# Branches of a hybrid decoder step in another order, and later use of what comes last at its seams

## The chip, the cores and the metric

The kernel runs on one core of a Trainium2 chip, as one launch. The metric is the device time in microseconds (us). Three runs of the kernel before gave 1140.0 (median), 1137.69 and 1142.15. The core has a tensor engine (PE; its weight loads are listed apart as PEld), a vector engine (DVE), a scalar engine (ACT), GpSimd (POOL) and SyncE (SP), which issues most loads. Each works through its own queue in order; the tensor engine's results go to PSUM, which DVE and ACT read.

## The reference

Two layers of a decoder trunk are run for a prompt of 256 tokens and for 8 samples of 4 tokens, 288 columns in all, with 1024 rows of model width. Cut to what matters here:

```
h  = rms(x)
q,k,v, x_b,y_b, q_c,k_c,v_c,r_c, a_c, g_a,g_b,g_c = split(h @ w_in)
o_a = window attention with sinks(q, k, v)                # branch a
o_b = gelu(y_b) * rg_lru(conv4(x_b))                      # branch b: a recurrence
o_c = rms(gla(q_c, k_c, v_c, a_c)) * silu(r_c)            # branch c: linear attention
x += (sig(g_a)*(o_a@Wa) + sig(g_b)*(o_b@Wb) + sig(g_c)*(o_c@Wc)) @ w_out
x += softmax(rms(x_q) rms(mem_k)) mem_v @ Wo              # 4 heads, 256 memory tokens
x += (silu(g) * val) @ w_down,  g,val = conv3(rms(x) @ w_up)
```

The three products with Wa, Wb, Wc are added up, and a sum has no order that the result depends on beyond rounding.

## The kernel before

Activations lie with the model dimension on partitions: X and its two halves xh and xl are eight blocks (k = 0 to 7) of 128 x 288. Each large product is made from three matmuls in fp32r (`mm3`, L213 to L215): xh by the weight's high half, xl by its high half, xh by its low half. A weight tile of 128 x 1024 is loaded by SP into `wst`, ACT writes its high half `whi` (L142) and DVE its low half `wlo` (L143). There are four `wst` and three each of `whi` and `wlo`. A tile of w_in feeds eight blocks k, so 24 matmuls; two tiles fill one two-bank PSUM buffer (`mm`, two of them). Four single banks (`sm`) serve everything small.

**What sets the order.** The queue of PE is the order in which the program is written. The chains of the three branches (`swa`, `gla`, `lru`), the norms and the memory's rms are generators: each `yield` hands back to the projections, and `tick` (L179) lets a chain take its next step when a running estimate of PE's time, `est["pe"]`, has passed the chain's `ready`. `account` adds to that estimate for each instruction: n/2400 us and 0.012 for an fp32r matmul, n/600 for one in fp32. A step becomes ready 0.3 us, plus what its yield gives, after the estimated end of the last. On DVE, ACT, POOL and SP a scheduler sets the order from priorities (`high_priority`) and its own estimates.

**A layer.** `mixers` makes the projections with the three chains interleaved; the recurrence's chain starts when linear attention's is past its states, and holds its exponentials (L744) until `swa` is done. Then come the gates (`gate(x)`, 4 x 2 tiles, x = 0 window attention, 1 recurrence, 2 linear attention) and the branch products (`branch(x)`, four pairs m = 0, 2, 4, 6, of 24 matmuls each). `branch` first calls `finish` on its chain. DVE multiplies the gate by the product out of PSUM (L1461); the sum `acc` is added on POOL for x = 1 and for the first two pairs of x = 2, on DVE for the last two (L1463); after x = 2 each pair is split into the halves `bh`, `bl` (L227 on ACT, L228 on DVE). `residual` multiplies them by w_out; its first pair of outputs takes k = 0 to 5 of both outputs first, then 6 and 7. `cross` is the cross-attention; it ends with the transposes of the probabilities (L1220), the samples' 64 small products (L1262), their transpose (L1268), the prompt's values (L1274) and the products with Wo. `ffn` is unchanged but for its first pair of products.

The wait for the window attention in the recurrence and the branches' order before:

```
        while not active["swa"].done:
            yield
...
        gate(0)
        gate(1)
        branch(0)
        gate(2, (0, 2, 4))
        branch(1, (0, 2))
```

Of the kernel before, what the change touches and what calls it, by code (L numbers as in the profile page):

```python
# [16 lines left out]
P = 128  # L17
# [49 lines left out]
def trunk(ctx: ExitStack, tc: tile.TileContext, a: dict):  # L67
# [82 lines left out]
    def account(i):  # L150

        if not hasattr(i, "engine") or not i.outs or i.opcode == "DMACopy":
            return
        e, n = str(i.engine), 1
        for _, c in i.outs[0].ap[1:]:
            n *= c
        if i.opcode == "Matmult":
            rows, cols = i.ins[0].ap[0][1], 1
            for _, c in i.ins[1].ap[1:]:
                cols *= c  # L160
            if i.ins[0].dtype == F32R:
                c = n / 2400 + 0.012
            elif getattr(i, "is_transpose", False):
                c = 0.109
            else:
                c = n / 600 * min(1.0, -(-rows // 32) / 4) * min(1.0, -(-cols // 32) / 4)
            est["pe"] += c
            if est["cur"] is not None:
                est["cur"] = max(est["cur"], est["pe"])
            return  # L170
        c = {"EngineType.DVE": 0.09 + n / 970, "EngineType.Activation": 0.12 + n / 1200}.get(e, 0.15 + n / 600)
        f = str(getattr(i, "func", "")).split(".")[-1]
        if i.opcode == "Activation" and f in TABLES and est["table"] not in TABLES[f]:
            est["table"] = TABLES[f][0]
            c += 1.28
        cur = est["cur"] if est["cur"] is not None and est["serial"] else est["pe"]
        t = est["busy"][e] = max(est["busy"].get(e, 0.0), cur) + c
        if est["cur"] is not None and not (est["serial"] and e == "EngineType.Pool"):
            est["cur"] = max(est["cur"], t + 0.1)  # L179
# [37 lines left out]
    def proj(out, src, nk, bh, bl):  # L217

        hi, lo = weights(src)
        for k in range(nk):  # L220
            w = slice(k * P, (k + 1) * P)
            mm3(out, hi[:, w], lo[:, w], bh(k), bl(k), k == 0, k == nk - 1)
            if k % 2:
                tick()

    def split(hi, lo, src):
        A.copy(hi, src)  # L227
# [72 lines left out]
    def head_norm(src, n, scale, nt=T, bw=TB):  # L300

        sq = s5()[:, : n * nt].rearrange("p (j t) -> p j t", t=nt)
        A.activation(sq, src, AF.Square)
        yield
        pss = psm()
        for j in range(n):
            PE.matmul(pss[32 * j : 32 * j + 32, :nt], cc("one32"), sq[:, j], start=True, stop=True, skip_group_check=True)
        yield
        ss = m1(nt)
        A.copy(ss[: 32 * n], pss[: 32 * n, :nt])  # L310
        yield
        nb = nt // bw
        pt = psm()
        for b in range(nb):
            PE.transpose(pt[:bw, b * P : b * P + 32 * n], ss[: 32 * n, b * bw : (b + 1) * bw], ident[: 32 * n, : 32 * n])
        yield
        cols = pt[:bw, : nb * P].rearrange("p (b j g) -> p b j g", j=4, g=32)[:, :, :n, 0]
        v = sm([P, 32], "rc")[:bw, : nb * n]
        V.tensor_copy(v.rearrange("p (b j) -> p b j", j=n), cols)
        r = rsqrt(v, [bw, nb * n], scale)  # L320
        yield
        return r
# [157 lines left out]
    def swa(l, got, Q, KV):  # L480
# [37 lines left out]

            V.scalar_tensor_tensor(x, x, prm[:, l, g : g + 1], bc(cc(c), n), ALU.mult, ALU.mult)

        yield
        pq, pg = flip(ss, 2, P), psm()
        for b in range(3):
            PE.transpose(pg[:TB, b * 32 : b * 32 + 32], sk[:, b * TB : (b + 1) * TB], ident[:32, :32])
# [110 lines left out]
        for kv in range(2):  # L635
            rows = slice(kv * 64, kv * 64 + 64)
            G.tensor_copy(qblk[rows, :, kv, :, :], Q[rows, :, NP_:T].rearrange("p j (b s) -> p b j s", s=NS))
        yield
        pscore = psm()
        for b in range(NB):  # L640
            r = 32 * (b % 4)
# [7 lines left out]
        for g in range(2):  # L649
            V.tensor_tensor_reduce(out=pt[:, g, :], in0=pscore[:, g * 132 : g * 132 + 132], in1=cc("ms"),  # L650
                                   scale=rqs[:, g : g + 1], scalar=-3e38, op0=ALU.add, op1=ALU.max, accum_out=mx[:, g : g + 1])
        yield
        sink = prm[:, l, C_SKS : C_SKS + 1]
        V.tensor_scalar(mx, mx, sink, -1.0, ALU.max, ALU.mult)
        A.activation(es, mx, AF.Exp, bias=sink)
        for g in range(2):
            A.activation(pt[:, g, :], pt[:, g, :], AF.Exp, bias=mx[:, g : g + 1], accum_out=den[:, g : g + 1])
        yield
        V.tensor_add(den, den, es)
        V.reciprocal(den, den)  # L660
        for g in range(2):
# [3 lines left out]
        for g in range(2):  # L665
            V.tensor_mul(pn[:, g], pt[:, g, P : P + NS].unsqueeze(1).to_broadcast([P, NB, NS]),
                         mb[:, g].unsqueeze(2).to_broadcast([P, NB, NS]))
        yield
        ptr = psm()
        for g in range(2):  # L670
            PE.transpose(ptr[:, g * P : (g + 1) * P], pt[:, g, :P], ident)
            PE.transpose(ptr[:32, (2 + g) * P : (3 + g) * P], pn[:, g].rearrange("p b s -> p (b s)"), ident)
        yield
        ptt = m1(2 * P)
        ptn = m1(2 * P)[:32]
        A.copy(ptt, ptr[:, : 2 * P])
        V.tensor_copy(ptn, ptr[:32, 2 * P : 4 * P])
        yield
        po = psm()
        for g in range(2):  # L680
            PE.matmul(po[:, g * P : (g + 1) * P], ptn[:, g * P : (g + 1) * P], vs, start=(g == 0), stop=False,
# [1 line left out]
        for b in range(NB):  # L683
            r, g = 32 * (b % 4), b // 4
            PE.matmul(po[r : r + 32, g * P : (g + 1) * P], ptt[:, b * 32 : b * 32 + 32], vc[:, b, :], start=False, stop=True,
                      skip_group_check=True)
        yield
        ot = m1(2 * P)
        A.copy(ot, po[:, : 2 * P])
        yield  # L690
        po = psm()
        for g in range(2):
            PE.transpose(po[:, g * P : (g + 1) * P], ot[:, g * P : (g + 1) * P], ident)
        yield
        os = m1(P).rearrange("p (j t) -> p j t", j=4)
        pov = po[:, : 2 * P].rearrange("p (b v j s) -> p v j b s", v=2, j=4, s=NS)
        for kv in range(2):
# [11 lines left out]
    def lru(l, got, xb, gy):  # L709
# [23 lines left out]
        for t in range(4):  # L733
            for g, (dst, c) in enumerate(((r, C_LBA), (ig, C_LBX))):
                pg = psm()
                PE.matmul(pg[:, :WO], wax[:, g * 4 + t, :], xc[:, t], start=True, stop=True)
                A.activation(dst[:, t], pg[:, :WO], AF.Sigmoid, bias=prm[:, l, c + t : c + t + 1])
            yield
        while not active["swa"].done:
            yield  # L740
        av, u = s5w(), s5w()
        for t in range(4):
# [282 lines left out]
    def mem_rms(sqs):  # L1025

        if sqs:
            pss = psm()
            for k, sq in enumerate(sqs):
                PE.matmul(pss[32 * k : 32 * k + 32, :NP_], cc("one32"), sq, start=True, stop=True, skip_group_check=True)  # L1030
            ss = m1(NP_)
            A.copy(ss, pss[:, :NP_])
            yield
            pt = flip(ss, 2, P)
            sr = sm([P, 3], "sr")[:, :2]
            V.tensor_reduce(sr, pt[:, :, :, 0], AX.X, ALU.add)
            V.tensor_copy(rm, rsqrt(sr, [P, 2], 1.0 / D))
            yield
            pb = psm()
            for b in range(2):  # L1040
                PE.transpose(pb[:, b * P : (b + 1) * P], rm[:, b : b + 1].to_broadcast([P, P]), ident)
            A.copy(rmb, pb[:, :NP_])
# [42 lines left out]
    def residual(srcs, nks, bh, bl, out=None):  # L1085

        for m in range(0, KD, 2):
# [8 lines left out]
                for k in range(nks[c]):  # L1096
                    todo.append((i, offs[c] + k, hi[:, k * P : (k + 1) * P], lo[:, k * P : (k + 1) * P]))
            if m == 0 and nk_all == KD:
                todo.sort(key=lambda t: t[1] >= 6)

            split_ = out is not None and m == KD - 2
            po = [psm(), psm()] if split_ else [pm[:, 0], pm[:, 1]]
# [33 lines left out]
    def cross(l, mem, mh, ml, kcs, vcs):  # L1136
# [74 lines left out]
        def flips(b):  # L1211
# [2 lines left out]
            V.reciprocal(dn, dn)  # L1214
            for h in range(4):
                V.tensor_scalar(pt[:, h], pt[:, h], dn[:, h : h + 1], None, ALU.mult)
            for m in range(2):
                ptr = psm()
                for h in range(4):
                    PE.transpose(ptr[:, h * P : (h + 1) * P], pt[:, h, m * P : (m + 1) * P], ident)  # L1220
                dst = ptt[m][:, :, ts]
# [42 lines left out]
                              skip_group_check=True)  # L1264
        os = m1(P)
        A.copy(os, po[:, :P])
        ptr = psm()
        PE.transpose(ptr[:, :P], os, ident)  # L1268
        split(oh[:, :, NP_:T], ol[:, :, NP_:T], ptr[:, :P].rearrange("p (h t) -> p h t", t=32))
        for h in (0, 2):  # L1270
            po = psm()
            for i in range(2):
                for m in range(2):
# [2 lines left out]
            po3 = po.rearrange("p (h t) -> p h t", t=NP_)  # L1276
            split(oh[:, h : h + 2, :NP_], ol[:, h : h + 2, :NP_], po3)

        for m in range(0, KD, 2):
            hi, lo = weights(a["wo"][l, m // 2], 0 if m == 2 else AHEAD)  # L1280
            pm = pmm()
            for i in range(2):
                for k in range(4):
                    w = slice(k * 256 + i * P, k * 256 + (i + 1) * P)
                    mm3(pm[:, i, :T], hi[:, w], lo[:, w], oh[:, k], ol[:, k], k == 0, k == 3)
            with tc.high_priority(AHEAD):
                V.tensor_add(X[:, m : m + 2], X[:, m : m + 2], pm[:, :, :T])


    def ffn(l):  # L1290
# [7 lines left out]
        def up(c, pm=None):  # L1298
            if pm is None:
                pm = pmm()  # L1300
                pm = (pm, pm[:, 0], pm[:, 1])
            for i in range(2):
                proj(pm[1 + i][:, :T], a["up"][l, 2 * c + i], KD, lambda k: xh[:, k, :], lambda k: xl[:, k, :])
            return pm
# [45 lines left out]
    def mixers(l):  # L1350
        chains, got = active, {}

        def win(i, n):
            pm = pmm()
            for j in range(n):
                proj(pm[:, j, :T], a["win"][l, i + j], KD, lambda k: xh[:, k, :], lambda k: xl[:, k, :])
            return pm
# [91 lines left out]
        def branch(x, ms=range(0, KD, 2)):  # L1449
            oh, ol = chains[("swa", "lru", "gla")[x]].finish()  # L1450
            for m in ms:
# [7 lines left out]
                g = gates[x, m]  # L1459
                with tc.high_priority(AHEAD):  # L1460
                    V.tensor_mul(g, g, pm[:, :, :T])  # L1461
                if x:
                    (G if x == 1 or m < KD - 4 else V).tensor_add(acc[m], acc[m], g)  # L1463
                else:
                    acc[m] = g
                if x == 2:
                    w = slice(m % 4, m % 4 + 2)
                    split(bh[m // 4][:, w], bl[m // 4][:, w], acc[m])

        gate(0)  # L1470
        gate(1)
        branch(0)
        gate(2, (0, 2, 4))
        branch(1, (0, 2))
        mh = [s5v(4, NP_, F32R), s5v(4, NP_, F32R)]
        ml = [s5v(4, NP_, F32R), s5v(4, NP_, F32R)]
        mem = active["mem"] = Chain(mem_load(l, mh, ml))
        gate(2, (6,))
        branch(1, (4, 6))
        branch(2)  # L1480
        kcs = [load_kc(l, b) for b in range(NB)]
        vcs = [load_vc(l, b, g2) for b in range(4)]
        residual(lambda m: [a["wout"][l, m]], (KD,), lambda k: bh[k // 4][:, k % 4], lambda k: bl[k // 4][:, k % 4])
# [194 lines left out]
```

## Time and profile before

| | |
|---|---|
| three runs | 1140.0 us (1137.69 to 1142.15) |
| the profiled execution | 1141.05 us, its span 1139.1 us |
| PE busy, PEld busy | 1107.9 us (97%), 1061.3 us (93%) |
| DVE, ACT, POOL busy | 794.3 us (70%), 629.8 us (55%), 252.4 us (22%) |
| mean granted clock of PE | 0.989 |
| HBM | 172 GB/s over the span |

The span runs from the first instruction to the last; 1.95 us of the profiled execution lie around it. Busy is the union of an engine's instructions. Matmuls overlap and their ends are modelled, so the pace is read from starts or from counts in a stretch. In the rows, `<-` in a wait names what ended it.

### The profile page before, as it was taken

How to read it: one execution, taken by the hardware profiler on the slowest of the kernel's cores; microseconds unless marked ns; L12 is line 12 of the kernel's file. 1: busy time of each engine (PE TensorE's matmuls, PEld its weight loads, DVE VectorE, ACT ScalarE, POOL GpSimd, SP SyncE). 2: the span in 40 equal slices, each digit the busy share in tenths (PEclk: the TensorE clock that was granted, in tenths of full speed). 3: DMA queues.
4: the chain of work that ended last, by engine and by line, in shares of the span. 5: the costliest groups of instructions: out<-in, count | busy, mean ns of one | idle time of the engine just before them, and what ended most of it. 6: DMA issues, size and time to landing. Idle time of an engine off the chain costs nothing. (4 is left out here: it accounts for less than half of the span.)

```text
span 1139.1 us, 22360 instructions
## 1 busy us (share of the span) xinstructions
PE 1107.9 (97%) x8846; PEld 1061.3 (93%) x8846; DVE 794.3 (70%) x1454; ACT 629.8 (55%) x971; POOL 252.4 (22%) x426
## 2 busy tenths in 40 slices
PE   9999997999999999999999999979999999999998
PEld 8898986999988999999999989869999899999998
DVE  6876866777765887885458769566776668878743
ACT  6545777535455656654346476864354456566532
POOL 1220101031111455550022100010311014555400
PEclk9999998999999999999999999989999999999999
DMA  8753453567466555556555435445675544455662
GB/s 279 266 181 115 152 179 116 187 201 242 150 221 234 148 167 161 155 162 197 172 170 180 138 103 178 160 141 166 203 242 166 187 142 150 167 160 158 184 193 84
DMA packets 62663, 198.11 MB, mean 174 GB/s; under 512 B 7960, under 2 KB 11768, under 8 KB 62560
## 3 DMA queue, kind: packets, MB, share of 16 engines
q1 hardware_dynamic: 59536, 188.55, 52.0%
q0 software_dynamic: 2880, 8.15, 1.9%
q8 instruction: 69, 1.13, 0.4%
q14 instruction: 34, 0.28, 0.1%
q10 hardware_dynamic: 144, 0.00, 0.0%
HBM read 187.35 MB, written 8.95 MB: 172 GB/s over the span
## 5 line engine op out<-in xcount | busy, mean ns | idle before, releaser
L142 ACT CAST whi<-wst 128x1024 fp32r<-128x1024 f32 (+1 forms) x302 | 312.5, 1036 | 302.1 <-PE mm L214 239.6
L143 DVE TENSOR_TENSOR wlo<-wst,whi 128x1024 fp32r<-128x1024 f32 (+1 forms) x302 | 373.6, 1238 | 143.1 <-ACT whi L142 141.5
L213 PE MATMUL mm<-xh,whi 128*128 128x288 f32 x1488 | 448.4, 301 | 0.0
L214 PE MATMUL mm<-xl,whi 128*128 128x288 f32 x1488 | 440.4, 296 | 1.0 <-DVE xl L264 1.0
L215 PE MATMUL mm<-xh,wlo 128*128 128x288 f32 x1488 | 439.8, 296 | 0.0
L213 PEld LDWEIGHTS mm<-xh,whi 128*128 128x128 f32 x1488 | 280.8, 189 | 12.0 <-issue 9.1
L214 PEld LDWEIGHTS mm<-xl,whi 128*128 128x128 f32 x1488 | 281.0, 189 | 2.6 <-DVE xl L264 1.9
L215 PEld LDWEIGHTS mm<-xh,wlo 128*128 128x128 f32 x1488 | 280.6, 189 | 0.4
L213 PE MATMUL mm<-s,whi 128*128 128x288 f32 (+1 forms) x756 | 226.3, 299 | 8.3 <-ACT s L227 7.4
L214 PE MATMUL mm<-s,whi 128*128 128x288 f32 (+1 forms) x756 | 225.5, 298 | 4.9 <-DVE s L228 4.9
L215 PE MATMUL mm<-s,wlo 128*128 128x288 f32 (+1 forms) x756 | 224.7, 297 | 0.0
L213 PEld LDWEIGHTS mm<-s,whi 128*128 128x128 f32 x756 | 144.8, 192 | 10.7 <-ACT s L227 7.9
L214 PEld LDWEIGHTS mm<-s,whi 128*128 128x128 f32 x756 | 145.0, 192 | 6.4 <-DVE s L228 6.3
L215 PEld LDWEIGHTS mm<-s,wlo 128*128 128x128 f32 x756 | 144.7, 191 | 0.6
L1329 DVE SCALAR_TENSOR_TENSOR y<-u,prm,y 128x304 f32<-128x304 f32 x176 | 83.6, 529 | 0.2
L1333 POOL TENSOR_TENSOR m<-y 128x256 f32<-128x256 f32 x44 | 61.0, 1386 | 70.3 <-ACT y L1330 61.3
L227 ACT CAST s<-m 128x288 fp32r<-128x288 f32 (+1 forms) x46 | 19.6, 426 | 73.7 <-POOL m L1334 73.7
L1327 ACT ACTIVATE y<-u,prm 128x304 f32<-128x304 f32 x88 | 51.9, 635 | 12.8 <-DVE u L1320 12.8
L228 DVE TENSOR_TENSOR s<-m,s 128x288 fp32r<-128x288 f32 (+1 forms) x46 | 20.7, 449 | 47.3 <-ACT s L227 47.3
L269 POOL TENSOR_TENSOR s<-s 128x288 f32<-128x288 f32 x20 | 17.7, 885 | 141.9 <-ACT s L268 141.9
L1313 POOL COPY u<-s 128x32 f32<-128x32 f32 x44 | 44.4, 1011 | 0.0
L1463 POOL TENSOR_TENSOR g<-g,g 128x576 f32<-128x576 f32 x12 | 20.9, 1738 | 79.9 <-DVE g L1461 79.9
(392 smaller groups left out, 1273.9 us busy)
## 6 DMA issues: line engine op xcount, KB each, us to landing
wst<-in_win SPq DMA_DIRECT2D x98, 512.0 KB, 3.5
wst<-in_up SPq DMA_DIRECT2D x88, 512.0 KB, 3.5
wst<-in_down SPq DMA_DIRECT2D x32, 512.0 KB, 3.7
wst<-in_wbr SPq DMA_DIRECT2D x24, 512.0 KB, 3.5
s<-in_mk SPq DMA_DIRECT2D x16, 512.0 KB, 5.6
wst<-in_wout SPq DMA_DIRECT2D x16, 512.0 KB, 4.0
wst<-in_down SPq DMA_DIRECT2D x16, 384.0 KB, 3.2
g<-in_mv SPq DMA_DIRECT2D x16, 256.0 KB, 3.3
```

Source lines behind the costliest of these rows:

```text
L142: A.copy(hi[:, :n], st[:, :n])
L143: (E or V).tensor_sub(lo[:, :n], st[:, :n], hi[:, :n].bitcast(F32))
L213: PE.matmul(out, wh, bh, start=first, stop=False)
L214: PE.matmul(out, wh, bl, start=False, stop=False)
L215: PE.matmul(out, wl, bh, start=False, stop=last)
L227: A.copy(hi, src)
L228: V.tensor_sub(lo, src, hi.bitcast(F32))
L1313: G.tensor_copy(us[:, :, :, 0:2], fhist[:, 2 * c : 2 * c + 2])
L1327: A.activation(y[:, i, :WFO], u[:, i, 2:], AF.Identity, scale=w[2], bias=prm[:, l, C_FCB + f : C_FCB + f + 1])
L1329: V.scalar_tensor_tensor(y[:, i, :WFO], u[:, i, j : j + WFO], w[j], y[:, i, :WFO], ALU.mult, ALU.add)
L1333: G.tensor_mul(h[:, :NP_], y[:, 0, :NP_], y[:, 1, :NP_])
L1463: (G if x == 1 or m < KD - 4 else V).tensor_add(acc[m], acc[m], g)
```

## The change

It does these things.

1. The gates and branches come as c, a, b: linear attention's product first, window attention's second, the recurrence's last. The recurrence no longer holds its exponentials until window attention is done. The sum is now added on POOL for window attention and for pair 0 of the recurrence, on DVE for its pairs 2, 4, 6, and it is split after the recurrence.
2. The estimate takes n/1200 for an fp32 matmul, and 12 yields (in window attention's norm and at its end, in the head norms, in the memory's rms) give 1.0.
3. `pair` makes the first two tiles after a norm together (first of `mixers` of layer 2, first of `ffn`): k = 0 to 5 of both, then 6 and 7 of both. The first pair of w_out takes k = 0 to 3, then 4 and 5, then 6 and 7.
4. At the end of `cross` the second half of the probabilities is transposed into an `mm` buffer, the values of heads 0 and 1 come before the samples' transpose, and the first two products with Wo take heads 0 and 1 of both, then 2 and 3 of both.

```
-                c = n / 600 * min(1.0, -(-rows // 32) / 4) * min(1.0, -(-cols // 32) / 4)
+                c = n / 1200 * min(1.0, -(-rows // 32) / 4) * min(1.0, -(-cols // 32) / 4)
...
+    def pair(out, srcs, bh, bl):
+        ws = [weights(src) for src in srcs]
+        for ks in (range(KD - 2), range(KD - 2, KD)):
+            for i, (hi, lo) in enumerate(ws):
+                for k in ks:
+                    w = slice(k * P, (k + 1) * P)
+                    mm3(out(i), hi[:, w], lo[:, w], bh(k), bl(k), k == 0, k == KD - 1)
+                    if k % 2:
+                        tick()
...
-        yield
+        yield 1.0
...
-        while not active["swa"].done:
-            yield
...
-                todo.sort(key=lambda t: t[1] >= 6)
+                todo.sort(key=lambda t: max(t[1] // 2, 1))
...
+            two = pmm() if b else None
             for m in range(2):
-                ptr = psm()
+                ptr = two[:, m] if b else psm()
...
+        values(0)
+        ptr = psm()
+        PE.transpose(ptr[:, :P], os, ident)
+        split(oh[:, :, NP_:T], ol[:, :, NP_:T], ptr[:, :P].rearrange("p (h t) -> p h t", t=32))
+        values(2)
...
+            for x, ks in ((0, (0, 1)), (1, (0, 1)), (0, (2, 3)), (1, (2, 3))) if m0 == 0 else ((0, range(4)), (1, range(4))):
+                products(x, ks)
...
-                if x:
-                    (G if x == 1 or m < KD - 4 else V).tensor_add(acc[m], acc[m], g)
+                if x < 2:
+                    (G if x == 0 or m == 0 else V).tensor_add(acc[m], acc[m], g)
...
-                if x == 2:
+                if x == 1:
...
+        gate(2)
         gate(0)
-        gate(1)
-        branch(0)
-        gate(2, (0, 2, 4))
-        branch(1, (0, 2))
+        branch(2)
+        gate(1, (0, 2, 4))
+        branch(0, (0, 2))
...
-        gate(2, (6,))
-        branch(1, (4, 6))
-        branch(2)
+        gate(1, (6,))
+        branch(0, (4, 6))
+        branch(1)
```

On PE, at window attention's end in layer 1, the rows before are these (L671 and L672 transpose the samples' probabilities, L681 and L685 multiply by the values, L693 transposes the result; `mm_2160` is a gate's product, `mm_2275` the first branch product, window attention's own):

```order
L671 MATMUL sm_2179<-cst,m_2076 128x128
L672 MATMUL sm_2179<-cst,pn_2148 32x128
...
L681 MATMUL sm_2212<-m_466,m_2191 128x128 x2
L685 MATMUL sm_2212<-s_2004,m_2190 32x128 x8
...
L693 MATMUL sm_2237<-cst,m_2229 128x128 x2
...
L213 MATMUL mm_2275<-s_848,whi_2270 128x288
L214 MATMUL mm_2275<-s_849,whi_2270 128x288
L215 MATMUL mm_2275<-s_848,wlo_2271 128x288
```

60 product matmuls stand between the scores (L643) and L671, 18 between L672 and L681, 12 between L685 and L693, 6 between L693 and the first branch product.

The same place in the changed kernel (`mm_2249`, `mm_2292` and `mm_2361` are linear attention's branch products, `mm_2400` a gate of the recurrence):

```order
L682 MATMUL sm_2209<-cst,m_2078 128x128
L683 MATMUL sm_2209<-cst,pn_2176 32x128
...
L213 MATMUL mm_2249<-s_1854,whi_2244 128x288
...
L692 MATMUL sm_2274<-m_466,m_2227 128x128 x2
L696 MATMUL sm_2274<-s_1990,m_2226 32x128 x8
L213 MATMUL mm_2292<-s_1854,whi_2287 128x288
...
L704 MATMUL sm_2374<-cst,m_2305 128x128 x2
...
L213 MATMUL mm_2400<-xh,whi_2402 128x288
```

Now 66 product matmuls and eight of the recurrence's gates stand between the scores and L682, 36 between L683 and L692, 60 between L696 and L704, and 156 between L704 and window attention's first product.

On DVE, the last branch of layer 2 and the start of w_out, before (product with the gate L1461, weight tile L143, low half of the split L228, sum L1463):

```order
L1461 TENSOR_TENSOR g_9088<-g_9088,mm_9430 128x2x288
L143 TENSOR_TENSOR wlo_9564<-wst_9562,whi_9563 128x1024
L228 TENSOR_TENSOR s_8020<-g_8263,s_8018 128x576
L1461 TENSOR_TENSOR g_9166<-g_9166,mm_9465 128x2x288
L1463 TENSOR_TENSOR g_8341<-g_8341,g_9166 128x2x288
L143 TENSOR_TENSOR wlo_9570<-wst_9568,whi_9569 128x1024
L228 TENSOR_TENSOR s_8021<-g_8341,s_8019 128x576
L1461 TENSOR_TENSOR g_9308<-g_9308,mm_9500 128x2x288
L143 TENSOR_TENSOR wlo_9626<-wst_9624,whi_9625 128x1024
L1463 TENSOR_TENSOR g_8427<-g_8427,g_9308 128x2x288
L228 TENSOR_TENSOR s_8021<-g_8427,s_8019 128x576
```

It starts here at pair 2; pair 2's sum is not on this queue, POOL makes it.

The same stretch in the changed kernel (L1489, L143, L239, L1491 in the same roles):

```order
L1489 TENSOR_TENSOR g_9084<-g_9084,mm_9425 128x2x288
L1491 TENSOR_TENSOR g_8234<-g_8234,g_9084 128x2x288
L143 TENSOR_TENSOR wlo_9563<-wst_9561,whi_9562 128x1024
L239 TENSOR_TENSOR s_8000<-g_8234,s_7998 128x576
L1489 TENSOR_TENSOR g_9161<-g_9161,mm_9464 128x2x288
L143 TENSOR_TENSOR wlo_9569<-wst_9567,whi_9568 128x1024
L1491 TENSOR_TENSOR g_8302<-g_8302,g_9161 128x2x288
L1489 TENSOR_TENSOR g_9303<-g_9303,mm_9499 128x2x288
L239 TENSOR_TENSOR s_8001<-g_8302,s_7999 128x576
L143 TENSOR_TENSOR wlo_9625<-wst_9623,whi_9624 128x1024
L1491 TENSOR_TENSOR g_8400<-g_8400,g_9303 128x2x288
L239 TENSOR_TENSOR s_8001<-g_8400,s_7999 128x576
```

Pair 2's sum has moved onto DVE, one instruction more; the product of pair 6 has moved ahead of pair 4's low half.

## Rows read from the trace of the kernel before

**Rows 1.** The page's engines: busy us, share of the span, instructions.

```profile
PE 1107.9 (97%) x8846; PEld 1061.3 (93%) x8846; DVE 794.3 (70%) x1454; ACT 629.8 (55%) x971; POOL 252.4 (22%) x426
```

**Rows 2.** Waits of PE: who, for what; us in total, times, longest.

```profile
PE mm L213 <- ACT s L227: 7.4, 2, 3.8
PE mm L214 <- DVE s L228: 4.9, 6, 1.9
PE sm L681 <- DVE m L677: 3.9, 2, 1.9
PE sm L671 <- DVE m L662: 2.6, 2, 1.3
PE sm L255 <- ACT m L1032: 1.8, 1, 1.8
PE sm L255 <- ACT m L514: 1.1, 1, 1.1
PE mm L214 <- DVE xl L264: 1.0, 4, 0.3
PE mm L213 <- DVE g L1461: 0.8, 1, 0.8
PE sm L307 <- ACT s L303: 0.8, 2, 0.4
PE sm L1268 <- ACT m L1266: 0.8, 2, 0.4
PE sm L1220 <- ACT s L1226: 0.7, 2, 0.4
```

**Rows 3.** Stretches of us: length, engines' busy us, instructions; PEclk, DMA.

```profile
core 0: us, PE busy (x) PEld busy (x) DVE busy (x) ACT busy (x) POOL busy (x), PEclk, DMA share, GB/s
43.22:46.63 3.41, 3.41 (x16) 3.41 (x15) 3.02 (x15) 1.14 (x2) 0.00 (x0) 0.50 0.97 327
190.00:196.82 6.82, 3.53 (x13) 3.21 (x14) 5.66 (x8) 1.78 (x3) 3.31 (x5) 0.50 0.23 80
261.68:265.09 3.41, 3.41 (x16) 3.41 (x15) 3.41 (x7) 1.37 (x2) 0.10 (x1) 0.50 0.81 235
746.37:749.78 3.41, 3.41 (x27) 2.77 (x26) 1.46 (x1) 2.54 (x4) 0.16 (x1) 0.50 0.66 169
756.61:763.43 6.82, 5.93 (x25) 5.93 (x25) 3.75 (x5) 1.39 (x2) 2.92 (x7) 0.50 0.56 223
400.00:420.00 20.00, 20.00 (x154) 20.00 (x153) 16.37 (x31) 11.89 (x18) 10.85 (x19) 1.00 0.50 168
```

**Rows 4.** Timeline of PE before L671: start, us, what, [idle, releaser].

```profile
177.30 0.29 PE L215 MATMUL mm<-xh,wlo 128*128 128x288 f32 x1
178.88 0.33 PE L671 MATMUL sm<-cst,m 128*128 128x128 f32 x1 [1.28 <-DVE m L662]
```

**Rows 5.** Groups by shape: count, busy us, mean ns, idle before.

```profile
L142 ACT CAST whi<-wst 128x1024 fp32r<-128x1024 f32 x286 | 299.3, 1048 | 286.2 <-PE mm L214 225.1 <-issue 24.7 <-ACT s L268 12.4
L143 DVE TENSOR_TENSOR wlo<-wst,whi 128x1024 fp32r<-128x1024 f32 x286 | 358.4, 1254 | 137.6 <-ACT whi L142 136.0
L1461 DVE TENSOR_TENSOR g<-g,mm 128x576 f32<-128x576 f32 x24 | 18.0, 749 | 8.3 <-PE mm L215 8.3
L1463 POOL TENSOR_TENSOR g<-g,g 128x576 f32<-128x576 f32 x12 | 20.9, 1738 | 79.9 <-DVE g L1461 79.9
L1463 DVE TENSOR_TENSOR g<-g,g 128x576 f32<-128x576 f32 x4 | 3.0, 758 | 0.1
L227 ACT CAST s<-g 128x576 fp32r<-128x576 f32 x8 | 5.4, 674 | 17.6 <-POOL g L1463 11.1 <-DVE g L1463 6.6
L228 DVE TENSOR_TENSOR s<-g,s 128x576 fp32r<-128x576 f32 x8 | 6.0, 756 | 8.9 <-ACT s L227 8.9
L747 DVE TENSOR_TENSOR s<-s,s 128x1248 f32<-128x1248 f32 x2 | 2.9, 1453 | 0.0
```

**Rows 6.** Line L228: min/median/max ns, first and last start us.

```profile
L228 DVE TENSOR_TENSOR s<-s,s x4: 1350/1359/1359, 154.5 to 762.5; 128x1152 fp32r<-128x1152 f32 x4
```

More of the change, by code (lines that the diff above doesn't have):

```diff
@@ L519, in turn @@
             V.scalar_tensor_tensor(x, x, prm[:, l, g : g + 1], bc(cc(c), n), ALU.mult, ALU.mult)
-        yield
+        yield 1.0
         pq, pg = flip(ss, 2, P), psm()
@@ L637, in swa @@
             G.tensor_copy(qblk[rows, :, kv, :, :], Q[rows, :, NP_:T].rearrange("p j (b s) -> p b j s", s=NS))
-        yield
+        yield 1.0
         pscore = psm()
@@ L651, in swa @@
                                    scale=rqs[:, g : g + 1], scalar=-3e38, op0=ALU.add, op1=ALU.max, accum_out=mx[:, g : g + 1])
-        yield
+        yield 1.0
         sink = prm[:, l, C_SKS : C_SKS + 1]
@@ L657, in swa @@
             A.activation(pt[:, g, :], pt[:, g, :], AF.Exp, bias=mx[:, g : g + 1], accum_out=den[:, g : g + 1])
-        yield
+        yield 1.0
         V.tensor_add(den, den, es)
@@ L667, in swa @@
                          mb[:, g].unsqueeze(2).to_broadcast([P, NB, NS]))
-        yield
+        yield 1.0
         ptr = psm()
@@ L672, in swa @@
             PE.transpose(ptr[:32, (2 + g) * P : (3 + g) * P], pn[:, g].rearrange("p b s -> p (b s)"), ident)
-        yield
+        yield 1.0
         ptt = m1(2 * P)
@@ L677, in swa @@
         V.tensor_copy(ptn, ptr[:32, 2 * P : 4 * P])
-        yield
+        yield 1.0
         po = psm()
@@ L686, in swa @@
                       skip_group_check=True)
-        yield
+        yield 1.0
         ot = m1(2 * P)
         A.copy(ot, po[:, : 2 * P])
-        yield
+        yield 1.0
         po = psm()
@@ L693, in swa @@
             PE.transpose(po[:, g * P : (g + 1) * P], ot[:, g * P : (g + 1) * P], ident)
-        yield
+        yield 1.0
         os = m1(P).rearrange("p (j t) -> p j t", j=4)
@@ L737, in lru @@
                 A.activation(dst[:, t], pg[:, :WO], AF.Sigmoid, bias=prm[:, l, c + t : c + t + 1])
-            yield
-        while not active["swa"].done:
             yield
@@ L1032, in mem_rms @@
             A.copy(ss, pss[:, :NP_])
-            yield
+            yield 1.0
             pt = flip(ss, 2, P)
@@ L1266, in cross, with values @@
         A.copy(os, po[:, :P])
[L1267 to L1270, printed above, removed]
+        def values(h):
             po = psm()
@@ L1277, in cross, with products @@
             split(oh[:, h : h + 2, :NP_], ol[:, h : h + 2, :NP_], po3)
[L1279 to L1287, printed above, removed]
+        values(0)
[3 more added lines that the diff above has]
+        values(2)
+        for m0 in range(0, KD, 4):
+            ms = (m0, m0 + 2)
+            ws = [weights(a["wo"][l, m // 2], 0 if m == 2 else AHEAD) for m in ms]
+            pms = [pmm(), pmm()]
+            def products(x, ks):
+                hi, lo = ws[x]
+                for i in range(2):
+                    for k in ks:
+                        w = slice(k * 256 + i * P, k * 256 + (i + 1) * P)
+                        mm3(pms[x][:, i, :T], hi[:, w], lo[:, w], oh[:, k], ol[:, k], k == 0, k == 3)
+            for x, ks in ((0, (0, 1)), (1, (0, 1)), (0, (2, 3)), (1, (2, 3))) if m0 == 0 else ((0, range(4)), (1, range(4))):
+                products(x, ks)
+                if ks[-1] == 3:
+                    with tc.high_priority(AHEAD):
+                        V.tensor_add(X[:, ms[x] : ms[x] + 2], X[:, ms[x] : ms[x] + 2], pms[x][:, :, :T])
     def ffn(l):
@@ L1301, in up @@
                 pm = (pm, pm[:, 0], pm[:, 1])
+            if c == 0:
+                pair(lambda i: pm[1 + i][:, :T], [a["up"][l, i] for i in range(2)], lambda k: xh[:, k, :], lambda k: xl[:, k, :])
+                return pm
             for i in range(2):
@@ L1354, in win @@
             pm = pmm()
+            if i == I_Q:
+                pair(lambda j: pm[:, j, :T], [a["win"][l, i + j] for j in range(2)], lambda k: xh[:, k, :], lambda k: xl[:, k, :])
+                return pm
             for j in range(n):
```

## The prediction

> **What bounds the kernel now.** I read the page's engine rows first. PE is busy 1107.9 of 1139.1 us; DVE, ACT and POOL have much more room [rows 1]. So the time is PE's queue: its work, the waits in it, and the clock at which it runs. In a stretch of the FFN 154 matmuls take 20 us, 0.130 us each [rows 3]; I use 0.132 for a product matmul (24 to a tile, 3.17 us). The change adds no matmul and removes none, so only waits and clock can move.
>
> Second, the waits of PE [rows 2]. The eleven rows add up to 25.8 us in 25 waits. Most of it is one place, met once a layer: the end of window attention. L671 waits for the normalised probabilities (2.6 us in two), L681 for their transposes' copies (3.9), then the first branch product for its high half (7.4) and, in most of the L228 row, for the low half. Each is a chain of small DVE and ACT steps with too few matmuls in between to cover it. The rest are seams: the memory's rms in w_out (L1032, 1.8), window attention's norm (L514, 1.1), xl at the first product after a norm (1.0), an `mm` buffer not yet read (L1461, 0.8), the head norms (0.8), and the end of the cross-attention (0.8 and 0.7).
>
> Third, what a wait costs beyond its idle time. Before L671, PE's starts are 1.58 us apart where the pace is 0.13, so 1.45 is lost for a gap of 1.28 [rows 4]: 0.17 more. And there are five stretches at granted clock 0.50, the 1.2 GHz level, against 1.00 elsewhere (2.4 GHz) [rows 3]. In 261.68:265.09 PE is busy throughout and holds 16 matmuls, counting those cut by the edges; at the FFN's pace it would be 26. In each case PE had sat in waits of this list just before the clock fell.
>
> The Trainium skill ("Trainium Kernel Development and Optimization", Performance Expectations) says that matmul busy time is a bad measure of the distance to the limit, and that the weight loads' busy share is a good one. By the matmul row at most 31.2 us could be won in all, and with the losses set off below the kernel would come to about 1118; by the weight loads' row, 1061.3, up to 77.8 us lie open. Rows 3 side with the weight loads: PE busy at half clock counts as busy.
>
> **Part by part.** The gross gain, if all that is listed went: idle 25.8 us; restarts 25 x 0.17 = 4.2 us; clock, half of PE's busy time in the slow stretches: 1.7 + 1.75 + 1.7 + 2.95 = 8.1, and for 746.37, where many of the 27 matmuls are small, between 0.5 and 1.7, say 1.2. Together 9.3, and in all 39.3 us.
>
> *Branches as c, a, b.* Between L704 and window attention's first product now stand 156 matmuls, 20.6 us, where 6 stood: the 7.4 us and their low halves are covered by the gates. Linear attention comes first instead. A split of its size first starts at 154.5 us [rows 6], 24 us before L671 [rows 4]; its product now stands 12 matmuls behind those transposes, so it is early by over 20 us. The recurrence comes last, some 400 matmuls (53 us) behind its last gate matmul, without the hold for window attention.
>
> *The steps of window attention.* L671 gets 66 matmuls and eight of the recurrence's gates instead of 60, at least 0.8 us more, against waits of 1.3. L681 gets 36 instead of 18: 2.4 us more against 1.9. But the recurrence's steps now fall among these on ACT and DVE (sigmoid and exponential take turns, and L747 alone holds DVE for 1.45 us [rows 5]), and evacuations queue behind them. In layer 1 DVE has such a step ahead of the read of a buffer that PE needs next. What that costs no row shows: between nothing and two of L747, 2.9 us; I take 1.2, in layer 1 alone.
>
> *The seam into w_out stays.* Per pair of the last branch DVE now does a weight tile, a product, a sum and a low half: 1.25 + 0.75 + 0.76 + 0.76 = 3.52 us [rows 5] against PE's 3.17. So DVE is the bound there. From the end of pair 0's product: product 0.75, POOL's sum 1.74 (2.3 with DVE busy beside it), cast 0.67, low half 0.76, handed on in 0.1 each: 4.7. Then on DVE, as the rows of the order list it, products, sums, tiles and low halves up to pair 6's sum: 3 x 0.75 + 3 x 0.76 + 3 x 1.25 + 2 x 0.76 = 9.8, so 14.5; its high half on ACT at 15.3, its low half at 16.1. PE needs 72 matmuls for the other three products and 36 of w_out to come to k = 6: 14.3 us. It waits 1.0 and 0.8. In layer 1 six short factor steps stand in DVE's queue too, and some factor matmuls in PE's: 1.5. With restarts 3.3 + 0.8 = 4.1 us come back; bounds 0 (the halves arrive earlier than my sum) and 6.
>
> *Yields and estimate.* The estimate runs slower past fp32 work, so steps come later in PE's queue. L1032's flip moves from the start of w_out to 12 matmuls in and has 24 behind the squares instead of 12: 1.6 us against 1.8 plus an ACT queue that is shorter there, gone. The head norms get 6 more (0.8 us) against 0.4 each, gone. L514 gets 6 more, 0.8 of 1.1: 0.3 stays.
>
> *`pair` and the end of the cross-attention.* `pair` puts 18 matmuls, 2.4 us, ahead of xl's blocks 6 and 7, for waits of 0.3. It needs the second tile after 18 matmuls instead of 24; the cast and low half of a tile take 1.05 + 1.25 [rows 5], and three buffers let them run ahead: cost 0 to 0.8 at each of three places, I take 0. In `cross` the values of two heads hide the copy before the samples' transpose, and `mm` buffers replace a bank that ACT was still reading: the 0.8 and 0.7 go, and so do the low-half waits at the first product with Wo, which now has 24 matmuls before heads 2 and 3.
>
> *Clock.* The seam's waits are about as long as those ahead of the slow stretches, so I leave one stretch of 3.41 us: 1.7 (0 to 3.4). For short waits that I have not seen, 0.7.
>
> Sum: 39.3 - 1.2 - 4.1 - 0.3 - 1.7 - 0.7 = 31.3 us. The profiled execution took 1141.05 us, 1.95 of it around the span, so 1109.7 by its measure. It lies 1.05 above the median of 1140.0; against that, 1109.
>
> **The rivals.**
>
> *Half comes back.* ACT and DVE are no faster, and the recurrence now shares the stretch with window attention's end. If new waits of some 2 us arise there in both layers, and the clock falls behind them, about half of window attention's waits (13.9 us in three rows and some 3 of L228's) and of its two slow stretches (4.7) returns: 11 to 12 us with restarts, so 1121 (1117 to 1130). For it: DVE busy 5.66 us in the 6.82 of 190.00 [rows 3]. Against it: in layer 2 the order leaves window attention's end further apart still.
>
> *All goes and the seam too:* 39.3 - 0.3 gives about 1101. Against it: DVE's 3.52 against 3.17 us.
>
> *The change doesn't do what it says.* The scheduler on DVE and ACT puts the late steps later as PE's queue grants more room, and the waits only move: 1137, within the noise. The rows of the order speak against it, since the first product's operand is another.
>
> *Slower.* The recurrence, last now, isn't ready: its place is the first product of `branch(1)`, its price one us for each us late, in each layer. It costs more than the change wins only when the chain runs over 53 + 16 = 69 us from its last gate matmul. The last of the four large splits, its own in layer 2, begins at 762.5 us [rows 6], before the slow stretch behind window attention's end is over [rows 3]: held back, it was still ready about as soon as window attention. 20 us late in each layer would make 1109 + 40 = 1149.
>
> **How the numbers follow.** Forecast 0.68 (own range 1101 to 1117), half 0.20, all 0.05, moved waits 0.05, slower 0.02. About 0.5% (5.7 us) is what a measurement here can tell from no change. Faster by more: 0.68 + 0.20 + 0.05 = 0.93; same 0.05; slower 0.02. The range of 8 in 10 runs from 1099, a little under the case where all goes, to 1124, which leaves out the moved waits, the slower case, and about half of the upper part of "half".
>
> **What would show it.** In the new profile: L682 and L692 without waits in layer 2 and with about a microsecond in layer 1; no wait of any branch's first product for ACT or DVE; waits for L239 at k = 6 of w_out's first pair, 1.5 to 1.8 us a layer; the list's sum at 5 to 8 us; slow stretches down from 23.9 us to 3 to 7; PE's busy time down by several us with the same matmul count. I am wrong if waits of 2 us or more stand at window attention's end, if `branch(2)` waits for linear attention, or if the slow stretches stay while the waits go.

## The result, and the profile after

The changed kernel takes 1108.5 us (median of 4 runs, 1108.1 to 1108.8) against 1140.2 for the kernel before on the same chip: a ratio of 0.9725, 95% interval 0.9713 to 0.9736. The forecast was 1109. The profiled execution took 1108.66 us against 1141.05, 32.4 less; its span is 1106.9 against 1139.1, 32.2 less.

The engines' row of the page, which answers to [rows 1]:

```profile
PE 1096.7 (99%) x8846; PEld 1054.2 (95%) x8846; DVE 794.4 (72%) x1456; ACT 623.1 (56%) x968; POOL 254.5 (23%) x424
```

PE has the same 8846 instructions and is busy 11.2 us less. So of the span's 32.2 us, 21.0 were PE standing idle and 11.2 were PE busy but slow (half clock and restarts). Waits of PE (who, for what; us in total, times, longest), which answer to [rows 2]; L433 belongs to the opening and was there before:

```profile
PE mm L1230 <- ACT s L1236: 1.7, 2, 0.8
PE sm L433 <- DVE warm L415: 1.2, 1, 1.2
PE sm L1070 <- DVE ry L259: 1.1, 2, 0.6
PE mm L214 <- DVE s L239: 0.8, 2, 0.4
PE mm L213 <- ACT s L238: 0.7, 1, 0.7
PE mm L213 <- DVE g L1470: 0.5, 1, 0.5
```

The first four rows of before, 18.8 us and nearly all of it window attention's end, are down to the 1.5 us of the `s` rows; no row has L682 or L692, and no product of a branch waits for its halves. What is left stands at k = 6 of w_out. L1230 and L1070 are new. Stretches of the changed kernel, to be held against [rows 3] (length, engines' busy us, PEclk, DMA); the second and the fourth hold the end of window attention in either layer:

```profile
43.22:46.63 3.41, 3.41 (x28) 3.41 (x28) 3.41 (x10) 1.14 (x2) 0.00 (x0) 1.00 1.02 389
176.00:196.82 20.82, 20.82 (x167) 20.16 (x167) 15.10 (x15) 19.12 (x30) 1.04 (x2) 1.00 0.62 200
261.68:265.09 3.41, 3.41 (x28) 3.41 (x28) 2.85 (x4) 1.58 (x2) 0.81 (x1) 1.00 0.53 190
740.00:763.00 23.00, 23.00 (x186) 22.71 (x182) 19.07 (x26) 15.43 (x24) 4.62 (x8) 1.00 0.63 210
```

In 3.41 us stand 28 matmuls where 16 stood at granted clock 0.50, and PE has no gap at window attention's end. The clock stays at 1.00, the 2.4 GHz level, through the whole span but its last 0.5 us.

### The profile page after: what moved, and what is told of

Its sections match the earlier page's. It is cut to its first block, busy times and chain, and to the rows that moved or that the text cites. A ratio compares the mean times of both kernels' runs of the same rounds, so it can differ in the third digit from the quotient of the medians.

```text
span 1106.9 us, 22351 instructions
## 1 busy us (share of the span) xinstructions
PE 1096.7 (99%) x8846; PEld 1054.2 (95%) x8846; DVE 794.4 (72%) x1456; ACT 623.1 (56%) x968; POOL 254.5 (23%) x424
## 4 chain that ended last, share of the span: by engine, by line
PE 91%; DVE 5%; ACT 2%; issue 1%; DMA 0%; POOL 0%; SPq 0%; ACTq 0%; DVEq 0%; POOLq 0%
PE mm L213 25%; PE mm L214 25%; PE mm L215 25%; DVE wlo L143 2%; PE sm L214 1%; PE sm L215 1%; PE sm L213 1%; ACT whi L142 1%; PE sm L747 1%; DVE xl L275 1%; PE mm L446 1%; PE sm L1086 1%; PE sm L1282 1%; PE mm L1210 1%; PE sm L1272 1%
## 5 line engine op out<-in xcount | busy, mean ns | idle before, releaser
L143 DVE TENSOR_TENSOR wlo<-wst,whi 128x1024 fp32r<-128x1024 f32 (+1 forms) x302 | 370.8, 1230 | 129.4 <-ACT whi L142 123.4
L213 PE MATMUL mm<-s,whi 128*128 128x288 f32 (+1 forms) x756 | 223.6, 296 | 1.3 <-ACT s L238 0.7
L214 PE MATMUL mm<-s,whi 128*128 128x288 f32 (+1 forms) x756 | 222.5, 294 | 0.8 <-DVE s L239 0.8
L213 PEld LDWEIGHTS mm<-s,whi 128*128 128x128 f32 x756 | 142.2, 188 | 3.6 <-issue 2.3
L214 PEld LDWEIGHTS mm<-s,whi 128*128 128x128 f32 x756 | 142.1, 188 | 1.3 <-DVE s L239 1.3
L215 PEld LDWEIGHTS mm<-s,wlo 128*128 128x128 f32 x756 | 142.3, 188 | 0.7 <-DVE wlo L143 0.3
L1352 ACT ACTIVATE y<-u,prm 128x304 f32<-128x304 f32 x88 | 52.0, 636 | 12.8 <-DVE u L1345 12.8
L239 DVE TENSOR_TENSOR s<-m,s 128x288 fp32r<-128x288 f32 (+1 forms) x46 | 20.7, 451 | 47.3 <-ACT s L238 47.3
L1341 DVE TENSOR_TENSOR u<-mm,rbc 128x512 f32<-128x512 f32 x42 | 28.7, 684 | 1.0 <-PE mm L215 1.0
```

The costliest lines, as they stand in the source:

```text
L143: (E or V).tensor_sub(lo[:, :n], st[:, :n], hi[:, :n].bitcast(F32))
L213: PE.matmul(out, wh, bh, start=first, stop=False)
L214: PE.matmul(out, wh, bl, start=False, stop=False)
L215: PE.matmul(out, wl, bh, start=False, stop=last)
L239: V.tensor_sub(lo, src, hi.bitcast(F32))
L1341: V.tensor_mul(u[:, :, 2 : 2 + NP_], pm[0][:, :, :NP_], bc(rbc[:, :NP_], 2))
```

## The experiments

Each was timed beside the kernel before, which took 1140.5 to 1142.3 us there; ratios are to that. The opening's waits (L433, L446) differ by up to 1.6 us between the profiled executions, so a verdict on less than that rests on the waits in the profile. The new order of w_out's first pair was not run by itself.

**The order alone, and everything but the order.** `order_alone` is the kernel before with the diff's hunks on `gate`, `branch`, the sums and the hold; `order_undone` is the changed kernel without them.

> The kernel before with the branches as c, a, b (sums and hold as in the new order) and nothing else. Theory: the order takes nearly all of window attention's waits (L671, L681, first product: some 17 us idle), 2.4 us of restarts and the three slow stretches there (5.9 us): 1114 to 1118, no wait over 1 us at L671 or L681. Rival: the planner's new estimate is what moves L671 and L681 apart; then 5 us or more stay at these lines and it takes 1121 to 1126.

> The changed kernel with branches, sums and hold as before; estimate, yields, pair and the cross-attention's end stay. Theory (terms add up): it keeps about 4 us of idle time, 1 of restarts and two slow stretches (3.4 us) from the smaller parts: 1130 to 1134. Rival: the small parts are worth nothing without the order: 1137 or more, its slow stretches still 20 us or more.

1115.5 us (0.9782, 0.9766 to 0.9797) and 1128.4 (0.9891, 0.9879 to 0.9904). The order alone brings 25.7 us, the rest alone 12.8; together they are worth some 32, so about 6 overlap. Waits of `order_alone`, then of `order_undone`:

```profile
PE sm L1039 <- DVE rm L1035: 2.4, 1, 2.4
PE mm L214 <- DVE s L228: 1.0, 3, 0.4
PE sm L681 <- DVE m L677: 0.8, 2, 0.4
```

```profile
PE sm L692 <- DVE m L688: 5.3, 2, 3.6
PE mm L213 <- ACT s L238: 5.0, 3, 2.7
PE sm L704 <- ACT m L700: 2.0, 2, 1.5
```

The order takes the big waits by itself; the planner is not what moves them apart. Without the order the later steps move part of window attention's wait down to L692 and L704, and shorten it: these rows, with L683 (0.4) and the low halves (1.0), add up to 13.7 us where the four rows of before had 18.8. The order takes these 5 us as well, and that is most of the overlap. `order_undone` is a little faster than its theory's range, though in the clock its rival was right: two half-clock stretches of 10.24 us remain (the first row is what PE did ahead of one):

```profile
176.00:182.96 6.96, 5.21 (x47) 4.26 (x45) 4.82 (x8) 6.91 (x11) 0.00 (x0) 1.00 0.70 226
182.97:193.21 10.24, 6.16 (x24) 5.73 (x25) 2.11 (x3) 7.73 (x15) 0.16 (x1) 0.50 0.31 104
```

And `order_alone` has a new wait of 2.4 us, with a stretch of 3.41 us at 0.50 behind it: L1039 sends the memory's rms back through PE, in w_out.

**Filling the waits of the kernel before.**

```
+    def idle(n):        # planner's estimate left as it was
+        pz = psm()
+        [PE.matmul(pz[:, :T], xh[:, 0, :P], xh[:, j % KD, :], ...) for j in range(n)]
     idle(8)  ahead of L671;  idle(13) ahead of L681;  idle(38) ahead of branch(0)'s products
```

> The kernel before with 8, 13 and 38 added product matmuls whose result nobody reads, in PE's queue right ahead of L671, L681 and the first branch product, each a little shorter than the waits there. No wait ends earlier. Theory: the granted clock falls because PE stood idle there, and half clock costs time: the slow stretches at 190, 746 and 756 us go, and the time falls by 5.9 us of clock and 1.4 of restarts to 1132 to 1135 although PE has 118 matmuls more to do. Rival: the slow stretches are only slow next to waits and hide in them; then 1139 to 1142.

1135.5 us (0.9959, 0.9944 to 0.9973): 118 more matmuls and 5.7 us less. The added ones, and a stretch that was at 0.50 before [rows 3]:

```profile
L182 PE MATMUL sm<-xh x118: 290/294/302, 175.8 to 751.8; 128*128 128x288 f32 x118
756.61:763.43 6.82, 6.29 (x48) 6.06 (x47) 5.55 (x7) 5.67 (x10) 0.05 (x1) 1.00 0.18 51
```

In the profiled execution all five slow stretches are gone, and 48 matmuls stand where 25 stood. Two of the five (43.22 and 261.68) had nothing filled right ahead of them, so not all of it is the edit's; but the mean granted clock of the six executions is 0.996 to 1.000, against 0.989 to 0.992 in the eleven of the kernel before beside them. So half clock costs time of its own, and where PE's idleness was filled it went. PE is busy 1113.8 us, 5.9 more than before, with 118 matmuls that take 15.6 us at 0.132: 9.7 us of its busy time, half clock and restarts, are gone. Two longer waits, 2.4 us (L1041 1.3, L435 1.1), hid part of that: the profiled execution fell by 6.4 us, to 1134.66.

**The planner and the hold.** `planner_undone`: `n / 600`, and every new `yield 1.0` a `yield`. `hold_kept`: `while not active["swa"].done: yield` put back.

> The changed kernel with the old estimate (n / 600) and plain yields. Theory: waits at L514 (1.1), L1043's flip (1.8) and the head norms (0.8) return with 0.7 of restarts and two slow stretches (3.4), against 1.5 us that the new wait at L1070 gives back: 1114 to 1118. Rival: with the new order there is enough other work at these places and the yields are worth nothing: 1108 to 1111.

> The changed kernel with the recurrence's hold for window attention put back. Theory: last in the order, it has some 50 us to spare, so the hold costs nothing, and window attention's end is undisturbed: 1107.5 to 1109. Rival: the recurrence is late at its first product, or its steps now crowd the seam: 1111 or more, with a wait of L213 at that product.

1114.5 us (0.9771, 0.9758 to 0.9783) and 1114.9 (0.9772, 0.9759 to 0.9786). The longest wait of each:

```profile
PE sm L1050 <- DVE rm L1046: 3.6, 1, 3.6
```

```profile
PE sm L1052 <- DVE rm L1048: 3.4, 1, 3.4
PE mm L214 <- DVE s L239: 2.6, 6, 0.6
```

The same transposes of the memory's rms as in `order_alone`, each time with a stretch of 3.41 us at 0.50 behind them. They stand 24 to 30 matmuls behind the rms's first transposes (L1043) in these three kernels; in the changed one 48, and nothing waits. In the kernel before they stood 30 behind as well, but at half clock, and did not wait; where the clock stayed up, in `waits_filled`, they waited 1.3. `planner_undone` hits its theory's range partly by luck: of the waits that it named, 0.9 at L514 (there L525) and 0.8 at the head norms came back, and the 3.6 stand in place of 1.8 at L1043 and of a second slow stretch. `hold_kept` comes out at the rival's time, but mostly not by its mechanism: the recurrence's last large split starts at 211.3 us in layer 1 against 209.1, and its first product waits for nothing; only the low halves at the seam wait longer, 2.6 us against 0.8. The hold shifts the planner's steps behind it (the memory's squares stand 36 matmuls further back), and nearly all the loss is in layer 1.

**`pair` and the end of the cross-attention.** `pair_undone`: every tile by `proj`. `cross_end`: flips, values and Wo as before. A run before it, `cross_undone`, put back by mistake the old `yield` in `mem_rms` and the old order of w_out's first pair as well.

> The changed kernel without pair. Theory: three waits of 0.3 us for xl return with their restarts, nothing else: 1109 to 1110.5. Rival: the second tile that pair asks for earlier costs PE as much or more: 1107.5 to 1108.7.

> The changed kernel with the cross-attention's end as before. Theory (prediction): the new end saves waits of 1.5 us at the copies, the low halves at Wo and restarts: undone, 1111 to 1112.5. Rival: the new wait at L1230 (1.7 us and two restarts in the changed kernel: the second four transposes into `two` stand until ACT has copied the first four) takes nearly all of it back: 1107.5 to 1109.5.

> The changed kernel with the end of the cross-attention alone as before (flips' tile, values and Wo's products; the run cross_undone had put back more than that). Theory, after that run: up to the values the new end wins nothing, since L1230's new wait costs what L1266's and L1226's did; only the low-half wait at Wo's first product returns, 0.6 us a layer: 1109 to 1110. Rival (prediction): 2 us or more: 1110.5 or more.

`pair_undone` takes 1114.1 us (0.9765, 0.9752 to 0.9778), far over both guesses: the waits for `xl` are up to 0.6 us long, those for `xh` are new, and in the profiled execution the clock falls behind them in layer 2. The other three executions kept a mean clock of 1.000 and took 1113.7 to 1114.6 all the same, so the clock is not needed for the loss.

```profile
PE mm L214 <- DVE xl L275: 1.9, 5, 0.6
PE mm L213 <- ACT xh L274: 1.4, 2, 0.7
```

```profile
895.20:898.81 3.61, 2.21 (x13) 1.52 (x12) 3.01 (x5) 1.60 (x4) 0.98 (x2) 1.00 0.72 249
898.81:902.22 3.41, 3.41 (x16) 3.41 (x16) 1.23 (x1) 0.98 (x1) 0.21 (x2) 0.50 0.53 145
```

`order_alone`, with the old end of the cross-attention and without `pair`, has four waits for `xl` of at most 0.3 and none of this kind for `xh`. The longer ones stand at the first product of `ffn` in both layers, right behind the cross-attention; those at the start of layer 2 are as before, 0.2 and 0.3. There the last sum into X comes late. PE's last product with Wo in layer 1 and DVE's sum of it into X, in `pair_undone`; DVE makes three blocks of `xl` in between:

```profile
342.85 0.29 PE L215 MATMUL mm<-s,wlo 128*128 128x288 f32 x1
...
345.30 0.74 DVE L1309 TENSOR_TENSOR X<-X,mm 128x576 f32<-128x576 f32 x1
```

The same in `cross_end`, which differs from the changed kernel in the old end alone:

```profile
345.25 0.29 PE L215 MATMUL mm<-s,wlo 128*128 128x288 f32 x1
345.95 0.74 DVE L1296 TENSOR_TENSOR X<-X,mm 128x576 f32<-128x576 f32 x1
```

From the start of the last product to the sum it is 2.45 us with the new end and 0.70 with the old one; the changed kernel and the other runs with the new end have the long way, `order_alone`, `cross_undone` and the kernel before the short one. So it is the new end, by its place the order of the products with Wo, that makes the norm's last halves late, and `pair` covers what this costs. The old end without `pair` was not run on the changed kernel.

`cross_undone` took 1112.4 us (0.9756, 0.9741 to 0.9772), 2.4 of it again a wait for the memory's rms. `cross_end` took 1109.0 (0.9716, 0.9692 to 0.9741), no difference that can be measured:

```profile
PE mm L214 <- DVE s L239: 1.5, 4, 0.4
PE sm L1277 <- ACT m L1275: 0.8, 2, 0.4
PE sm L1229 <- ACT s L1235: 0.7, 2, 0.4
```

The waits that the new end removes are here, 2.2 us with the two more low halves; the 1.7 us of L1230 is not. They nearly cancel. (Its profiled execution, the slowest of the five, has a wait of 1.2 for a weight's low half at 226.9 us as well, far from this place.)

**Where the sums of the last branch run.** One expression in `branch`: `m == 0` becomes `m < KD - 4` (`sums_pool`) or goes, all on V (`sums_dve`).

> The changed kernel with pair 2's sum of the last branch on POOL again, as before. Theory (prediction): DVE is the bound of this stretch (3.52 us a pair against PE's 3.17), so 0.76 us less for it gives 0.5 to 1.5 us: 1107 to 1108. Rival: what counts is how long a sum takes; pair 0's took POOL 2.49 us and DVE then stood idle 2.03 us for it, so a second one on POOL costs 0.5 to 2 us: 1109 to 1111.

> The changed kernel with pair 0's sum of the last branch on DVE as well (0.76 us instead of 2.49 on POOL). Theory: DVE no longer stands idle 2.0 us behind it, so the high and low halves at k = 6 of w_out come earlier and the seam's 1.6 us of waits shrink or go: 1106.5 to 1108. Rival (prediction's reading, DVE the bound there): one more sum on DVE delays what follows by 0.76 us: 1109 to 1110.5.

1110.0 us (0.9729, 0.9716 to 0.9743) and 1106.3 (0.9692, 0.9667 to 0.9716). The first cannot be told from the changed kernel; its profile has the seam's waits, 1.3 us, and a new one of 0.8 for an `mm` buffer that DVE reads late (L1489). The second's interval just touches that kernel's, but its profile has lost the seam's waits but for one of 0.2. The changed kernel's seam in layer 1, from pair 0's product on: POOL, DVE, then PE at k = 6 (start, us, what, [idle, releaser]):

```profile
236.24 2.49 POOL L1491 TENSOR_TENSOR g<-g,g 128x576 f32<-128x576 f32 x1 [1.90 <-DVE g L1489]
```

```profile
235.35 0.74 DVE L1489 TENSOR_TENSOR g<-g,mm 128x576 f32<-128x576 f32 x1
...
239.47 0.76 DVE L239 TENSOR_TENSOR s<-g,s 128x576 fp32r<-128x576 f32 x1 [2.03 <-ACT s L238]
240.15 0.75 DVE L1489 TENSOR_TENSOR g<-g,mm 128x576 f32<-128x576 f32 x1
...
250.72 0.75 DVE L239 TENSOR_TENSOR s<-g,s 128x576 fp32r<-128x576 f32 x1
```

```profile
250.28 0.29 PE L215 MATMUL mm<-s,wlo 128*128 128x288 f32 x1
250.69 0.40 PE L213 MATMUL mm<-s,whi 128*128 128x288 f32 x1
251.53 0.40 PE L214 MATMUL mm<-s,whi 128*128 128x288 f32 x1 [0.44 <-DVE s L239]
251.77 0.30 PE L215 MATMUL mm<-s,wlo 128*128 128x288 f32 x1
```

And in layer 2, DVE and PE:

```profile
783.17 0.74 DVE L1489 TENSOR_TENSOR g<-g,mm 128x576 f32<-128x576 f32 x1
...
787.21 0.76 DVE L239 TENSOR_TENSOR s<-g,s 128x576 fp32r<-128x576 f32 x1 [2.04 <-ACT s L238]
...
796.54 0.75 DVE L1491 TENSOR_TENSOR g<-g,g 128x576 f32<-128x576 f32 x1
798.03 0.76 DVE L239 TENSOR_TENSOR s<-g,s 128x576 fp32r<-128x576 f32 x1 [0.74 <-ACT s L238]
```

```profile
797.08 0.29 PE L215 MATMUL mm<-s,wlo 128*128 128x288 f32 x1
798.05 0.40 PE L213 MATMUL mm<-s,whi 128*128 128x288 f32 x1 [0.68 <-ACT s L238]
798.84 0.40 PE L214 MATMUL mm<-s,whi 128*128 128x288 f32 x1 [0.40 <-DVE s L239]
799.08 0.29 PE L215 MATMUL mm<-s,wlo 128*128 128x288 f32 x1
```

In both layers DVE stands idle 2.0 us for POOL's sum and the cast behind it. Only then does it work without a pause (in layer 2 from 787.21 to 797.29, with 0.2 us idle). So DVE's work alone doesn't set the end of this stretch: the wait for POOL that starts it late is worth more to PE's waits than the 0.76 us that a sum costs DVE, as `sums_dve` shows.

**The two new waits, and a better kernel.** `flips_first`:

```
+            ptrs = [two[:, m] if b else psm() for m in range(2)]
             for m in range(2):          # all eight transposes
                 ...
             for m in range(2):          # then the copies
         r = yield from head_norm(km, 4, 1.0 / P, NP_, P)
+        yield 0.5
```

`best` is this and `sums_dve` together.

> The changed kernel with all eight transposes of `two` ahead of ACT's and DVE's copies, and one more step of 0.5 us ahead of the memory keys' factor transposes (L1070), which puts these 12 matmuls later. Theory: L1230's and L1070's waits go, 1.7 + 1.1 us and four restarts (0.7): 1104.5 to 1105.5. Rival: the copies only end later and the next readers wait for them: 1107.5 to 1109.

> The edits of flips_first and sums_dve together on the changed kernel. Theory: their waits lie in different stages, so their gains add: 1108.5 less 3.3 less 2.2, 1102.5 to 1104. Rival: the earlier seam brings the memory keys' norm and the copies of the probabilities against DVE and ACT sooner, and half of it is lost: 1104.5 to 1106.

What stands at L1230 in the changed kernel, PE and ACT, and in `flips_first` PE (now L1231):

```profile
321.42 0.60 PE L1230 MATMUL mm<-cst,s 128*128 128x128 f32 x4
322.86 0.66 PE L1230 MATMUL mm<-cst,s 128*128 128x128 f32 x4 [0.84 <-ACT s L1236]
```

```profile
319.62 2.22 ACT L142 CAST whi<-wst 128x1024 fp32r<-128x1024 f32 x2
...
322.22 0.58 ACT L1236 COPY s<-mm 128x512 f32<-128x512 f32 x1
```

```profile
321.35 1.04 PE L1231 MATMUL mm<-cst,s 128*128 128x128 f32 x8
```

The second four start 0.06 us after ACT has read the first four's half of the tile, though they write the other half, and ACT's copy stood behind two weight casts. Written ahead of the copy they run through. `flips_first` takes 1105.2 us (0.9682, 0.9657 to 0.9707), without waits at L1231 or the keys' factors; `best` takes 1103.1 (0.9661, 0.9647 to 0.9676), by the medians 5.4 less than the changed kernel where 5.5 were added up, by the ratios some 7. Its longest wait outside the opening is 0.5 us.

## Why the prediction was right, and where not

**The frame held.** PE's queue is the kernel; waits, restarts and clock were the three terms. Forecast for the profiled execution 1109.7, measured 1108.66. The list of waits in full went from 27.5 us, opening included, to 6.4: 21.1 us less idle, where 25.8 - 5.5 (1.2 + 3.3 + 0.3 + 0.7) = 20.3 was forecast. PE's busy time fell by 11.2, forecast 4.2 - 0.8 of restarts and 9.3 - 1.7 of clock, 11.0. The Trainium skill ("Trainium Kernel Development and Optimization", Performance Expectations) is borne out on its point: the span fell by 32.2 us, more than the 31.2 that PE's matmul row left open, and `best` by 39.0 (to 1100.1). What the rows show behind it is that busy time at half clock and in restarts counts as busy.

**The order** did what was said, shown alone by `order_alone`. The recurrence was never late in a run in which it came last.

**Window attention's end in layer 1**, 1.2 us given back: nothing was. The long step that I feared (L747, here L756) did stand on DVE right ahead of the read of an `mm` buffer, from 178.48 us, but PE has no gap in 176.00:196.82.

**The seam**, 4.1 us: 1.5 in three waits and 0.5 of restarts. The end that I added up was about right: from the start of pair 0's product on DVE to the end of pair 6's low half the sum has 16.0 us, and it took 16.1 in layer 1 (235.35 to 251.47) and 15.6 in layer 2 (783.17 to 798.79). Two errors in it were small: DVE starts the next instruction before the last one's time is over (239.47 to 240.15, 0.68 us, for an instruction of 0.76), and POOL's sum took 2.49 where I had 2.3. What was sized too large is the loss. PE's starts at k = 6, three steps of 0.13, lose 1.6 us in layer 2 (forecast 1.8) and 1.1 in layer 1 (forecast 1.5), and that holds the restarts, for which I put 0.8 on top. The step that failed is the reading "DVE is the bound there": by it more work on DVE costs, and `sums_dve`, with a sum more on DVE, has all but lost the waits. `sums_pool`, with a sum less, has them still.

**Clock**: right that it goes, wrong that one stretch stays; the seam's short waits left it at 1.00. The 9.3 us was somewhat high: I took half of PE's busy time in the slow stretches, but there product matmuls start 0.24 us apart against 0.132, which loses 45%, so some 8.4. `waits_filled`, with 9.7 for clock and restarts, agrees. Two rows of the kernel before, from 261.68:265.09:

```profile
262.30 0.45 PE L215 MATMUL mm<-s,wlo 128*128 128x288 f32 x1
262.54 0.45 PE L213 MATMUL mm<-s,whi 128*128 128x288 f32 x1
```

**The yields**: L1032's wait and the head norms' went, and L514's 0.3 too. What I did not see: the rms' second visit to PE stands a step later in the same chain, and the order alone makes it a wait of 2.4 us. The later steps and the new estimate together are worth 6 us, not the 1.8 + 0.8 + 0.8 that I counted.

**`pair`** cost nothing, as taken, but is worth 5.6 us in the changed kernel, not three waits of 0.3: the cross-attention's new end makes the norm's last halves later. So much of its worth is another edit's cost, which the prediction put at nothing. **The cross-attention's end** was costed at a gain of 1.5 us and the low halves; the 0.8 and 0.7 did go, but the step that failed is that the `mm` buffer costs nothing. The operands were looked at and not the tile: L1230's new wait, 1.7 us, took nearly all of it back. L1070's wait, 1.1 us, is the price of the later steps or the new estimate, since `planner_undone` lacks it; I had them down as a gain only. Against 0.7 for unseen waits stand 2.8 at these two lines. So misses of 5.3 us (1.2 + 2.1 + 0.3 + 1.7) on one side were met by some 3 on the other (2.8 - 0.7, 0.7 of restarts there, 0.5 at L1470) and by 0.9 of clock put too high: that the total came within about 1 us is in part luck.

## What to carry to other kernels

Where an engine is full, price an order's edits by what stands late behind each wait, and look for the next visit of the same chain: a step moved to cover one wait uncovers another. Halves of one on-chip tile shared by two engines are one thing to wait for in this kernel, so write both before either is read. Before calling a helper engine the bound of a stretch, look for its own idle time there: gaps of 2.0 us pointed to POOL, and the run without POOL's sum bore it out in its waits. An edit may only pay for another one, as `pair` does for the order at Wo: undo them together as well as one by one.

## What the runs showed of the hardware that was not expected

A wait's cost in clock isn't read from its length. In the profiled execution of `waits_filled`, waits of 1.8 and 1.3 us at the memory's rms left the clock at 1.00, where before a wait of 1.8 there was followed by half clock [rows 2, 3]. A wait of 2.4 us at its second transposes was followed by half clock in `order_alone`, and not in the profiled execution of `cross_undone`. In `pair_undone` PE stood idle 1.4 of the 3.61 us ahead of a fall. Nor is it the same in each execution of a kernel: the mean granted clock of `waits_filled` was 0.996 in the one that took 1139.2 us and 1.000 in the one that took 1134.5. At 0.50 a product matmul started every 0.24 us in the rows above, not every 0.26.
